# A list scheduler in the kernel sets the order of all work in a cross-covariance attention

## The chip, the cores and the metric

One core of one Trainium2 chip runs the kernel. Its engines are PE (matmul; PEld is its weight load), DVE (vector), ACT (scalar), POOL (GpSimd) and SP, which issues all the DMA transfers. Each engine works through its own instructions in the order in which the program gives them and waits on semaphores for the others. The metric is the device time of one execution in microseconds.

## The reference

Q, K and V have the shape 8 x 12 x 512 x 64 (batch, heads, sequence, dimension) in float32. The attention is over the dimension, not over the sequence: each head has a 64 x 64 matrix.

```python
Q_norm = Q / (np.linalg.norm(Q, axis=-2, keepdims=True) + 1e-10)
K_norm = K / (np.linalg.norm(K, axis=-2, keepdims=True) + 1e-10)
attn = np.einsum('bhnd,bhne->bhde', Q_norm, K_norm)
attn = np.exp(attn - np.max(attn, axis=-1, keepdims=True))
attn = attn / (np.sum(attn, axis=-1, keepdims=True) + 1e-10)
return np.einsum('bhnd,bhde->bhne', V, attn).astype(np.float32)
```

## The kernel before

The 96 heads form 24 units of 4 heads, and two units form a pair `s` (12 pairs). A unit's Q, K or V is one transfer of 512 KB: 128 partitions, 32 for each head, with 16 rows of 64 in each. A pair's result leaves in two stores of 512 KB. That makes 96 transfers, 24 each of Q, K, V and the output, all in SP's queue.

For a unit, DVE casts Q and K to bf16, side by side in one tile (L77). PE multiplies that tile by its own transpose, 64 small matmuls (L89), so that each head's 128 x 128 Gram matrix holds Q^T Q, K^T K and K^T Q. [...] DVE takes the diagonals (L99) and K^T Q (L104) out of it. For a pair, DVE sums the diagonals (L108), GpSimd raises them to the power -1/2 (L110), DVE scales K^T Q by the norms of K (L114), PE transposes the result into the logits (L121, L122), ACT takes the exponential with the norms of Q as its scale (L128) and adds up the rows, and DVE divides (L134, L137), which gives `ab`.

V goes another way. GpSimd casts it to bf16 (L81), PE transposes it in two halves for a pair (L148) through one PSUM buffer, and ACT copies each half to SBUF (L152). Then PE multiplies by `ab` in four groups for a pair (L163), ACT copies each group from PSUM into the tile that is stored (L164), and after every second group SP stores the tile (L72).

The order is written out by hand. The main loop has 28 steps. Step `s` issues the loads of Q and K for unit s + 4 and of V for unit s + 2, then one store of pair s // 2 - 2, and then the compute, where unit s is in its grams, the pair before it in logits to output products, and the pair before that in its last output group. The program order of each engine is the order of these calls:

```python
if s + LA < U:
    load_qk(s + LA)
if s + LA - VLAG < U:
    load_v(s + LA - VLAG)
```

Of the kernel before, what the change touches and what calls it, by code (L numbers as in the profile page):

```python
# [13 lines left out]
D = 64  # L14
T = 16
HU = 4
J = T // 2


@with_exitstack  # L20
def kernel(
# [11 lines left out]
    S = U // 2  # L33

# [9 lines left out]

    const = ctx.enter_context(tc.tile_pool(name="const", bufs=1))
    qp = ctx.enter_context(tc.tile_pool(name="qp", bufs=5))
    vp = ctx.enter_context(tc.tile_pool(name="vp", bufs=4))
    vbp = ctx.enter_context(tc.tile_pool(name="vbp", bufs=4))
    qkp = ctx.enter_context(tc.tile_pool(name="qkp", bufs=3))
    vtp = ctx.enter_context(tc.tile_pool(name="vtp", bufs=2))  # L50
    sop = ctx.enter_context(tc.tile_pool(name="sop", bufs=6))
    small = ctx.enter_context(tc.tile_pool(name="small", bufs=2))
    ps_g = ctx.enter_context(tc.tile_pool(name="ps_g", bufs=1, space=bass.MemoryType.PSUM))
# [4 lines left out]
    qk32, v32, vb, qkb, gram, scr, kq, r8, kqs, lg, ex, ab, vt, so = ({} for _ in range(14))  # L58
    LO, HI = slice(0, D), slice(D, 2 * D)

    def load_qk(u):
        t_ = qk32[u] = qp.tile([128, 2, T, D], F32, name="qk32")
        r = u % 2
        nc.sync.dma_start(out=t_[:, r], in_=Qu[u * 128:(u + 1) * 128])
        nc.sync.dma_start(out=t_[:, 1 - r], in_=Ku[u * 128:(u + 1) * 128])

    def load_v(u):
        t_ = v32[u] = vp.tile([128, T, D], F32, name="v32")
        nc.sync.dma_start(out=t_, in_=Vu[u * 128:(u + 1) * 128])

    def store(s, i):
        nc.sync.dma_start(out=Of[s, i], in_=so[s, i])  # L72

    def cast_qk(u):
        t_ = qkb[u] = qkp.tile([128, T, 2 * D], BF16, name="qkb")
        for x in range(2):
            nc.vector.tensor_copy(t_[:, :, x * D:(x + 1) * D], qk32[u][:, x])  # L77

    def cast_v(u):
        t_ = vb[u] = vbp.tile([128, T, D], BF16, name="vb")  # L80
        nc.gpsimd.tensor_scalar(out=t_, in0=v32[u], scalar1=1.0, scalar2=0.0, op0=ALU.mult, op1=ALU.add)  # L81
# [24 lines left out]
    def norms(s):  # L106
        n2 = small.tile([128, 2 * HU], F32, name="n2")
        nc.vector.tensor_reduce(out=n2, in_=scr[s], axis=mybir.AxisListType.X, op=ALU.add)  # L108
        t_ = r8[s] = small.tile([128, 2 * HU], F32, name="r8")
# [21 lines left out]
    def normalise(s):  # L131
# [3 lines left out]
        a = ab[s] = abs_[s % len(abs_)]  # L135
# [5 lines left out]
    def vtrans(s, k):  # L141

        ps = ps_v.tile([128, 2, J // 2, 128], BF16, name="vps")
# [5 lines left out]
        if k == 0:  # L149
            vt[s] = vtp.tile([128, J, 128, 2], BF16, name="vt")  # L150
        o = vt[s][:, k * (J // 2):(k + 1) * (J // 2)]
        nc.scalar.copy(o.rearrange("p j x c -> p c j x"), ps)  # L152

    def outs(s, x):
        i, k = divmod(x, 2)
        if k == 0:
            so[s, i] = sop.tile([128, 2, J, D], F32, name="so")
        po = ps_o.tile([128, J // 2, 2, D], F32, name="po")
        for j in range(J // 2):
            for e in range(2):  # L160
                h = 2 * i + e
                w = vt[s][:, k * (J // 2) + j, 32 * h:32 * (h + 1), :].rearrange("p x c -> p (x c)")
                nc.tensor.matmul(po[e * D:(e + 1) * D, j].rearrange("p r d -> p (r d)"), w, ab[s][:, h, :])  # L163
        nc.scalar.copy(so[s, i][:, :, k * (J // 2):(k + 1) * (J // 2)].rearrange("p r j d -> p j r d"), po)  # L164

    LA = 4
    VLAG = 2

    for u in range(LA):
        load_qk(u)  # L170
        if u >= VLAG:
            load_v(u - VLAG)

# [10 lines left out]
    for i in range(3):  # L184
# [4 lines left out]
    cast_qk(0)  # L189
    for s in range(U + 4):  # L190
        p, odd = divmod(s, 2)
        if s + LA < U:
            load_qk(s + LA)
        if s + LA - VLAG < U:
            load_v(s + LA - VLAG)

        if odd and 0 <= p - 2 < S:
            store(p - 2, 1)
        if not odd and 0 <= p - 2 < S:
            store(p - 2, 0)  # L200
        if s + 1 < U:
            cast_qk(s + 1)
        if 0 <= s - 1 < U:
            cast_v(s - 1)
        if not odd and 0 <= p - 1 < S:
            scale_k(p - 1)
        if odd and 0 <= p - 1 < S:
            normalise(p - 1)
        if s < U:
            grams(s)  # L210
            squares(s)
        if odd and s < U:
            norms(p)
        if not odd and 0 <= p - 2 < S:
            outs(p - 2, 3)
        if not odd and 0 <= p - 1 < S:
            logits(p - 1)
            exps(p - 1)
            vtrans(p - 1, 0)
        if odd and 0 <= p - 1 < S:  # L220
            vtrans(p - 1, 1)
            for x in range(3):
                outs(p - 1, x)
# [30 lines left out]
```

## Time and profile before

| | |
|---|---|
| median of 3 runs | 140.41 us (140.38 to 140.78) |
| the profiled execution | 141.48 us, of which the span is 139.7 |
| PE, PEld | 84.4 us (60%), 69.6 us (50%) busy |
| DVE | 95.4 us (68%) |
| ACT | 71.9 us (51%) |
| POOL | 50.0 us (36%) |
| DMA | 50.69 MB, 363 GB/s over the span |
| mean granted TensorE clock | 0.82 |

The span is the time from the first to the last instruction of the profiled execution; what lies around it belongs to the launch. A busy share is a mean over the whole span: no engine is busy all the time, and the stretches of the span must be looked at one by one. L12 is line 12 of the kernel before.

### The profile page before, as it was taken

The numbers are of one execution on the slowest core, as the hardware profiler recorded it, in microseconds if no ns is written. First come the engines' busy times: TensorE is split into PE (matmuls) and PEld (weight loads), VectorE is DVE, ScalarE is ACT, GpSimd is POOL, SyncE is SP. The second block draws the span as 40 slices with busy tenths as digits, with TensorE's granted clock in tenths as the row PEclk, the third lists the DMA queues.
The fourth block names the chain that finished last, engine by engine and source line by source line (L and its number), as shares of the span: only waits on it lengthen the run. The fifth ranks groups of instructions, "written<-read, shape, count | busy, mean of one in ns | idle before, by whom it ended". The sixth has DMA issues, their size and how long they took to land.

```text
span 139.7 us, 5665 instructions
## 1 busy us (share of the span) xinstructions
PE 84.4 (60%) x2496; PEld 69.6 (50%) x2496; DVE 95.4 (68%) x183; ACT 71.9 (51%) x169; POOL 50.0 (36%) x45
## 2 busy tenths in 40 slices
PE   0225584795565954656966557946937745966440
PEld 0224473774454843545854446735835634855330
DVE  2347786798798867848797977886795977543200
ACT  0000047657386467344477636447573753865670
POOL 3002542740914705501906407308209209143000
PEclk9999999559999599855699985797797799686555
DMA  4999999999999999999999999999999999707016
GB/s 156 364 409 418 407 409 405 412 407 406 407 412 409 419 406 411 415 412 411 410 418 408 416 409 410 419 413 416 406 415 410 411 413 349 274 22 292 11 69 232
DMA packets 16920, 50.69 MB, mean 363 GB/s; under 512 B 1536, under 2 KB 1536, under 8 KB 16896
## 3 DMA queue, kind: packets, MB, share of 16 engines
q1 hardware_dynamic: 16896, 50.34, 90.8%
q8 instruction: 19, 0.31, 0.9%
q14 instruction: 5, 0.04, 0.1%
HBM read 37.75 MB, written 12.58 MB: 360 GB/s over the span
## 4 chain that ended last, share of the span: by engine, by line
PE 40%; ACT 22%; issue 13%; DVE 10%; POOL 5%; DMA 5%; SPq 1%; POOLq 0%; ACTq 0%
PE gram L89 15%; ACT vt L152 14%; PE po L163 9%; PE vps L148 8%; PE lg L121 7%; ACT ex L128 6%; POOL r L110 5%; DMA qk<-in_K_dram 5%; DVE kqs L114 3%; DVE scr L99 2%; DVE n L108 1%; DVE ab L137 1%; DVE kq L104 1%; ACT L128 1%; ACT so L164 1%
## 5 line engine op out<-in xcount | busy, mean ns | idle before, releaser
L89 PE MATMUL gram<-qkb 32*128 32x128 bf16 x1536 | 37.1, 259 | 21.3 <-issue 10.3
L110 POOL TENSOR_TENSOR r<-n,mhalf 128x8 f32<-128x8 f32 x12 | 23.2, 1932 | 57.6 <-DVE n L108 38.0
L89 PEld LDWEIGHTS <-qkb 32*128 32x128 bf16 x1536 | 30.2, 115 | 23.7 <-issue 10.8
L152 ACT COPY vt<-vps 128x1024 bf16<-128x1024 bf16 x24 | 31.2, 1301 | 16.4 <-PE vps L148 16.4
L164 ACT COPY so<-po 128x512 f32<-128x512 f32 x48 | 26.9, 587 | 22.7 <-PE po L163 22.2
L77 DVE CAST qkb<-qk 128x1024 bf16<-128x1024 f32 x48 | 32.3, 712 | 6.6 <-DMA qk<-in_K_dram 3.8
L163 PE MATMUL po<-ab,vt 128*64 128x128 bf16 x384 | 23.7, 257 | 17.4 <-ACT vt L152 13.3
L81 POOL TENSOR_SCALAR vb<-v 128x1024 bf16<-128x1024 f32 x24 | 25.8, 1078 | 18.6 <-DMA v<-in_V_dram 17.4
L163 PEld LDWEIGHTS <-vt 128*64 128x64 bf16 x384 | 16.3, 130 | 20.5 <-ACT vt L152 15.5
L99 DVE SCALAR_TENSOR_TENSOR scr<-gram,eye 64x256 f32<-64x256 f32 x48 | 20.2, 421 | 7.8 <-PE gram L89 7.3
L148 PE MATMUL vps<-identb,vb 128*64 128x128 bf16 x384 | 18.8, 251 | 8.7 <-ACT vt L152 7.7
L114 DVE TENSOR_TENSOR kqs<-kq,r 128x256 f32<-128x256 f32 x12 | 14.2, 1186 | 12.6 <-POOL r L110 12.6
L148 PEld LDWEIGHTS <-vb 128*64 128x64 bf16 x384 | 14.9, 128 | 12.3 <-issue 10.3
L128 ACT ACTIVATE ex<-lg,r 128x64 f32<-128x64 f32 x48 | 14.4, 311 | 5.7 <-PE lg L122 5.4
L121 PEld LDWEIGHTS lg<-eye,kqs 64*64 64x64 f32 x96 | 9.1, 181 | 9.0 <-DVE kqs L114 8.4
L121 PE MATMUL lg<-eye,kqs 64*64 64x64 f32 x96 | 11.0, 276 | 3.5 <-DVE kqs L114 3.5
L128 ACT ACT_TABLE_LOAD x1 | 1.3, 1283 | 19.3 <-PE lg L122 19.3
L122 PE MATMUL lg<-eye,kqs 64*64 64x64 f32 x96 | 11.0, 276 | 0.0
L137 DVE TENSOR_TENSOR ab<-ex,rinv 64x256 bf16<-64x256 f32 x24 | 10.3, 429 | 0.6
L104 DVE COPY kq<-gram 64x256 f32<-64x256 f32 x24 | 10.0, 419 | 0.4
L128 ACT ACTIVATION_READ_ACCUMULATOR ex<-lg,r 128x1 f32 x48 | 9.7, 202 | 0.0
L122 PEld LDWEIGHTS lg<-eye,kqs 64*64 64x64 f32 x96 | 9.1, 181 | 0.0
(12 smaller groups left out, 12.8 us busy)
## 6 DMA issues: line engine op xcount, KB each, us to landing
qk<-in_Q_dram SPq DMA_DIRECT2D x24, 512.0 KB, 10.1
qk<-in_K_dram SPq DMA_DIRECT2D x24, 512.0 KB, 10.1
v<-in_V_dram SPq DMA_DIRECT2D x24, 512.0 KB, 10.0
out_dram<-so SPq DMA_DIRECT2D x24, 512.0 KB, 10.0
```

What stands on the lines that cost most here:

```text
L77: nc.vector.tensor_copy(t_[:, :, x * D:(x + 1) * D], qk32[u][:, x])
L81: nc.gpsimd.tensor_scalar(out=t_, in0=v32[u], scalar1=1.0, scalar2=0.0, op0=ALU.mult, op1=ALU.add)
L89: nc.tensor.matmul(g[:, h, 0:2 * D], x, x, start=(t == 0), stop=(t == T - 1))
L99: nc.vector.scalar_tensor_tensor(out=scr[s][half, HU * (x ^ r):HU * (x ^ r) + HU], in0=g[half, :, half], scalar=1e-20, in1=eye2[half, None ...
L110: nc.gpsimd.tensor_tensor(out=t_, in0=n2, in1=mhalf, op=ALU.pow)
L121: nc.tensor.matmul(l[LO, h, :], kqs[s][HI, h, :], eye2[HI])
L122: nc.tensor.matmul(l[HI, h, :], kqs[s][LO, h, :], eye2[LO])
L128: nc.scalar.activation(e[:, h, :], lg[s][:, h, :], AF.Exp, scale=r8[s][:, h:h + 1], accum_out=z[:, h:h + 1])
L148: nc.tensor.transpose(ps[r * D:(r + 1) * D, c, j, :], vb[2 * s + r][:, t, :], identb)
L152: nc.scalar.copy(o.rearrange("p j x c -> p c j x"), ps)
L163: nc.tensor.matmul(po[e * D:(e + 1) * D, j].rearrange("p r d -> p (r d)"), w, ab[s][:, h, :])
L164: nc.scalar.copy(so[s, i][:, :, k * (J // 2):(k + 1) * (J // 2)].rearrange("p r j d -> p j r d"), po)
```

## The change

The hand-written loop goes. Every step becomes a piece with a key, the engines on which it may run with a cost in us for each, the pieces that must have ended (`after`), those that must have begun (`behind`), and a rank. A planner in the kernel, when the program is built, repeatedly takes the pieces that may begin within 0.25 us of the earliest one, and of these the one with the lowest rank, and then emits all pieces in the order of their planned beginnings. DMA is modelled as one queue with 8 transfers under way, 2.0 us of flight and 1.27 us for each transfer.

The ranks of transfers go with their unit's number: Q and K at 0.76 u / 24, V at 0.10 + 0.80 v / 24, stores 0.10 behind V's formula. Some buffers are added: V in bf16 6 for 4, transposed V 3 for 2, store tiles 8 for 6. The scaling of K^T Q moves from DVE to GpSimd, into one piece with the power. In the last four pairs (`s >= BOTH`), the copies of transposed V are halved and go to ACT or DVE, as do the copies of the output groups, and V's cast may go to DVE. The last two pairs (`s >= TAIL`) use other PSUM buffers: the Gram tile's four banks are closed after the last squares and opened again as two buffers for transposes and two for products.

```diff
+    HOP = 0.15
+    SLACK = 0.25
+    QUEUE = 8
+    FLIGHT = 2.0
...
+                for eng, cost in engines.items():
+                    begin = max(ready, free.get(eng, 0.7))
+                    if eng == "DMA":
+                        if len(landed) >= self.QUEUE:
+                            begin = max(begin, landed[-self.QUEUE])
+                        done = max(begin + self.FLIGHT, landed[-1] if landed else 0.0) + cost
+                        busy = begin + 0.45
...
+            first = min(b[0] for b in best)
+            begin, rank, key, (_, _, busy, eng, done) = min(
+                (b for b in best if b[0] <= first + self.SLACK), key=lambda b: (b[1], b[0], str(b[2])))
...
+    TAIL = S - 2
+    BOTH = S - 4
...
+    NB = dict(qk=5, v=4, vb=6, qkb=3, vt=3, so=8, sm=2, ab=3)
...
+    def late_pool():
+        if not late:
+            grams_only.close()
+            late["p"] = ctx.enter_context(tc.tile_pool(name="ps_t", bufs=2, space=bass.MemoryType.PSUM))
+        return late["p"]
...
-    def scale_k(s):
         t_ = kqs[s] = small.tile([128, HU, D], F32, name="kqs")
-        nc.vector.tensor_tensor(
+        nc.gpsimd.tensor_tensor(
             out=t_, in0=kq[s], in1=r8[s][:, HU:, None].to_broadcast([128, HU, D]), op=ALU.mult,
         )
...
-    cast_qk(0)
-    for s in range(U + 4):
...
+    QK_PACE, V_FROM, V_PACE, ST_LAG = 0.76, 0.10, 0.80, 0.10
+    def v_at(v):
+        return V_FROM + V_PACE * v / U
...
+        at = QK_PACE * u / U
+        free = [back("cq", u, NB["qk"], 0), back("cq", u, NB["qk"], 1)]
+        piece(("lq", u), {"DMA": X}, free, [back("lk", u, 1)], at, load_qk, u, 0)
+        piece(("lk", u), {"DMA": X}, free, [("lq", u)], at, load_qk, u, 1)
+        piece(("cq", u, 0), {"DVE": 0.70}, [("lq", u), back("gr", u, NB["qkb"])], [back("cq", u, 1, 1)], 10 + u, cast_qk, u, 0)
+        piece(("cq", u, 1), {"DVE": 0.70}, [("lk", u)], [("cq", u, 0)], 10 + u, cast_qk, u, 1)
+        piece(("gr", u), {"PE": 1.6}, [("cq", u, 0), ("cq", u, 1), back("sq", u, 1)], [], 2, grams, u)
+        piece(("sq", u), {"DVE": 1.30}, [("gr", u), back("sc", s, NB["sm"])], [back("sq", u, 1)], 1, squares, u)
...
+        piece(("rd", s), {"DVE": 0.69}, [("sq", 2 * s), ("sq", 2 * s + 1), back("sc", s, NB["sm"])], [], 1, sums, s)
+        piece(("sc", s), {"POOL": 2.4}, [("rd", s), back("lg", s, NB["sm"]), back("ex", s, NB["sm"])], [], 1, powers, s)
+        piece(("lg", s), {"PE": 0.8}, [("sc", s), back("ex", s, 1)], [], 1, logits, s)
+        piece(("ex", s), {"ACT": 2.05}, [("lg", s), back("nm", s, NB["sm"])], [], 1, exps, s)
+        piece(("nm", s), {"DVE": 1.05}, [("ex", s)] + [back("ou", s, NB["ab"], x) for x in range(4)], [], 1, normalise, s)
...
+        piece(("lv", v), {"DMA": X}, [back("cv", v, NB["v"])], [back("lv", v, 1)], v_at(v), load_v, v)
+        piece(("cv", v), {"POOL": 1.05, "DVE": (0.7, 0.2)} if s >= BOTH else {"POOL": 1.05},
+              [("lv", v), back("vt", v // 2, NB["vb"] // 2, 1)], [back("cv", v, 1)], 3 + 0.01 * v, cast_v, v)
...
+            if t:
+                wait = [("vc", s - 1, k, c) for c in halves] if s > TAIL else [("sq", U - 1)]
...
+            piece(("vc", s, k, c), {"ACT": 0.66, "DVE": 0.60} if s >= BOTH else {"ACT": 1.31},
...
+            wait = [("oc", n // 4 + (TAIL if t else 0), n % 4)] if n >= 0 else [("sq", U - 1)] if t else []
+            piece(("ou", s, x), {"PE": 0.5}, [("vc", s, k, c) for c in halves] + [("nm", s)] + wait, order, 3 + 0.01 * s, outs, s, x)
...
+            piece(("oc", s, x), {"ACT": 0.6, "DVE": (0.6, 0.2)} if s >= BOTH else {"ACT": 0.6}, [("ou", s, x)] + free, order, 2 + 0.01 * s, ocopy, s, x)
...
+            piece(("st", s, i), {"DMA": X}, [("oc", s, 2 * i), ("oc", s, 2 * i + 1)], order, v_at(2 * s + i) + ST_LAG, store, s, i)
+    for emit, eng in plan.run():
+        emit(eng)
```

In this code `U` is 24 and `S` 12, and `back(kind, i, n)` names the piece of that kind n numbers earlier, so it stands for a buffer's earlier use. The pieces are `lq`, `lk`, `lv` (loads), `cq`, `cv` (casts), `gr` (grams), `sq` (squares and the copy of K^T Q), `rd` (sums), `sc` (power and scaling), `lg`, `ex`, `nm` (logits, exponentials, division), `vt`, `vc` (transposes of V and their copies), `ou`, `oc` (output products and their copies) and `st` (stores).

## Rows read from the trace of the kernel before

**Rows 1.** The page's second part: 40 equal slices of the span.

```profile
DMA  4999999999999999999999999999999999707016
GB/s 156 364 409 418 407 409 405 412 407 406 407 412 409 419 406 411 415 412 411 410 418 408 416 409 410 419 413 416 406 415 410 411 413 349 274 22 292 11 69 232
```

**Rows 2.** Stretches: length, busy us of five engines, PEclk, DMA share, GB/s.

```profile
0.00:115.00 115.00, 71.06 (x2188) 58.74 (x2190) 86.61 (x167) 58.14 (x138) 43.27 (x40) 0.85 1.01 402
115.00:139.70 24.70, 13.32 (x312) 10.87 (x311) 8.77 (x17) 13.71 (x32) 6.76 (x5) 0.67 0.48 181
...
15.00:115.00 100.00, 67.05 (x2060) 55.25 (x2054) 79.21 (x152) 58.14 (x138) 40.93 (x30) 0.83 1.03 411
...
137.00:138.00 1.00, 0.00 (x0) 0.00 (x0) 0.00 (x0) 0.00 (x0) 0.00 (x0) 0.50 1.01 385
138.00:138.50 0.50, 0.00 (x0) 0.00 (x0) 0.00 (x0) 0.00 (x0) 0.00 (x0) 0.50 0.71 262
```

**Rows 3.** Timeline of SP, 95 us to the end: start, duration, instruction.

```profile
102.29 0.33 SPq L65 DMA_DIRECT2D qk<-in_K_dram  x1
...
108.67 0.33 SPq L69 DMA_DIRECT2D v<-in_V_dram  x1
109.98 26.39 SPq L72 DMA_DIRECT2D out_dram<-so  x7
```

**Rows 4.** The page's sixth part: issues, KB each, median us to landing.

```profile
qk<-in_K_dram SPq DMA_DIRECT2D x24, 512.0 KB, 10.1
```

**Rows 5.** Waits of SP before 108 us, then after: us, times, longest.

```profile
SPq L72 <- ACT so L164: 0.7, 3, 0.4
...
SPq L72 <- ACT so L164: 22.6, 6, 7.5
```

**Rows 6.** Timeline of the tail: start, duration, instruction, idle before it.

```profile
120.00 1.89 PE L89 MATMUL gram<-qkb 32*128 32x128 bf16 x64
...
123.36 0.69 DVE L108 TENSOR_REDUCE n<-scr 128x8 f32<-128x512 f32 x1
124.22 1.64 POOL L110 TENSOR_TENSOR r<-n,mhalf 128x8 f32<-128x8 f32 x1 [4.97 <-DVE n L108]
...
125.83 1.04 POOL L81 TENSOR_SCALAR vb<-v 128x1024 bf16<-128x1024 f32 x1
125.89 1.25 DVE L114 TENSOR_TENSOR kqs<-kq,r 128x256 f32<-128x256 f32 x1 [1.84 <-POOL r L110]
...
129.97 0.85 DVE L137 TENSOR_TENSOR ab<-ex,rinv 64x256 bf16<-64x256 f32 x2
130.96 1.06 PE L148 MATMUL vps<-identb,vb 128*64 128x128 bf16 x16 [1.64 <-ACT vt L152]
...
132.06 1.29 ACT L152 COPY vt<-vps 128x1024 bf16<-128x1024 bf16 x1 [1.15 <-PE vps L148]
...
134.72 0.64 PE L163 MATMUL po<-ab,vt 128*64 128x128 bf16 x8 [0.23 <-ACT so L164]
...
135.40 0.58 ACT L164 COPY so<-po 128x512 f32<-128x512 f32 x1 [0.24 <-PE po L163]
```

**Rows 7.** The same timeline, PE's groups at the full clock.

```profile
115.69 1.07 PE L89 MATMUL gram<-qkb 32*128 32x128 bf16 x64
116.69 0.41 PE L163 MATMUL po<-ab,vt 128*64 128x128 bf16 x7
...
119.43 0.64 PE L148 MATMUL vps<-identb,vb 128*64 128x128 bf16 x16
```

**Rows 8.** Groups by line, and lines L114 and L110 (ns min/median/max).

```profile
L77 DVE CAST qkb<-qk 128x1024 bf16<-128x1024 f32 x48 | 32.3, 712 | 6.6 <-DMA qk<-in_K_dram 3.8
...
L179 POOL TENSOR_TENSOR eye<-ident 128x64 f32<-128x64 f32 x1 | 0.3, 318 | 0.0
...
L114 DVE TENSOR_TENSOR kqs<-kq,r x12: 425/1254/1257, 17.6 to 125.9; 128x256 f32<-128x256 f32 x12
...
L110 POOL TENSOR_TENSOR r<-n,mhalf x12: 1635/1918/2169, 15.6 to 124.2; 128x8 f32<-128x8 f32 x12
```

More of the change, by code (lines that the diff above doesn't have):

```diff
@@ L17, with __init__, add, run @@
 J = T // 2
+LO, HI = slice(0, D), slice(D, 2 * D)
+class Order:
+    HOP = 0.15
+    SLACK = 0.25
+    QUEUE = 8
+    FLIGHT = 2.0
+    def __init__(self):
+        self.pieces = {}
+    def add(self, key, engines, after, behind, rank, emit):
+        after, behind = (tuple(a for a in x if a is not None) for x in (after, behind))
+        self.pieces[key] = (engines, after, behind, rank, emit)
+    def run(self):
+        end, begun, free, landed, order = {}, {}, {}, [], []
+        todo = dict(self.pieces)
+        while todo:
+            best = []
+            for key, (engines, after, behind, rank, _) in todo.items():
+                if any(a not in end for a in after + behind):
+                    continue
+                ready = max([end[a] + self.HOP for a in after] + [begun[a] for a in behind], default=0.7)
+                pick = None
+                for eng, cost in engines.items():
[5 more added lines that the diff above has]
+                        busy = begin + 0.45
+                    else:
+                        bias = 0.0
+                        if isinstance(cost, tuple):
+                            cost, bias = cost
+                        done = busy = begin + cost
+                        done += bias
+                    if pick is None or done < pick[0]:
+                        pick = (done, begin, busy, eng, done if eng == "DMA" else busy)
+                best.append((pick[1], rank, key, pick))
+            first = min(b[0] for b in best)
+            begin, rank, key, (_, _, busy, eng, done) = min(
+                (b for b in best if b[0] <= first + self.SLACK), key=lambda b: (b[1], b[0], str(b[2])))
+            end[key] = done
+            begun[key] = begin
+            free[eng] = busy
+            if eng == "DMA":
+                landed.append(done)
+            order.append((begin, len(order), key, eng))
+            del todo[key]
+        self.end = end
+        self.order = sorted(order)
+        return [(self.pieces[key][4], eng) for _, _, key, eng in self.order]
 @with_exitstack
@@ L56 @@
     ps_o = ctx.enter_context(tc.tile_pool(name="ps_o", bufs=2, space=bass.MemoryType.PSUM))
[L58 to L65, printed above, removed]
+    grams_only = ExitStack()
@@ new lines, with copy @@
+    ps_g = grams_only.enter_context(tc.tile_pool(name="ps_g", bufs=1, space=bass.MemoryType.PSUM))
+    late = {}
+    def late_pool():
[3 more added lines that the diff above has]
+        return late["p"]
+    qk32, v32, vb, qkb, gram, scr, kq, r8, kqs, lg, ex, ab, vps, vt, po, so = ({} for _ in range(16))
+    def copy(eng, o, i):
+        if eng == "ACT":
+            nc.scalar.copy(o, i)
+        elif eng == "DVE":
+            nc.vector.tensor_copy(o, i)
+        else:
+            nc.gpsimd.tensor_scalar(out=o, in0=i, scalar1=1.0, scalar2=0.0, op0=ALU.mult, op1=ALU.add)
@@ L183 @@
     abs_ = []
-    for i in range(3):
+    for i in range(NB["ab"]):
         a = const.tile([128, HU, 2 * D], BF16, name=f"ab{i}")
@@ L187 @@
         abs_.append(a)
-    cast_qk(0)
-    for s in range(U + 4):
[L191 to L223, printed above, removed]
+    plan = Order()
@@ new lines, with piece, back @@
+    X = 1.27
+    QK_PACE, V_FROM, V_PACE, ST_LAG = 0.76, 0.10, 0.80, 0.10
+    def v_at(v):
+        return V_FROM + V_PACE * v / U
+    def piece(key, engines, after, behind, rank, fn, *args):
+        if key[0] in ("cv", "vc", "oc"):
+            plan.add(key, engines, after, behind, rank, lambda eng: fn(eng, *args))
+        else:
+            plan.add(key, engines, after, behind, rank, lambda eng: fn(*args))
+    def back(kind, i, n, *rest):
+        return (kind, i - n, *rest) if i - n >= 0 else None
```

105 lines of the change are left out of this document (70 added, 35 removed).

## The prediction

> **What bounds the kernel now.** I read first the page's slices [rows 1], to find the stretches with different limits. The reader is to see the DMA row at 9 (90% or more) from slice 2 to slice 34 and then broken, 7 0 7 0 1 6, while the GB/s row falls from about 410 to 274, 22, 292, 11, 69, 232. So there are two kernels in one: a stream that the DMA engines set, and a tail of some 22 us that something else sets. The split into stretches gives sizes [rows 2]: 411 GB/s at a share of 1.03 from 15 to 115 us, and 181 GB/s over the last 24.7 us. The traffic is the same 96 transfers of 0.524 MB whatever their order (0.524 MB / 411 GB/s = 1.28 us each). What is left at 115 us is 24.7 us x 181 GB/s = 4.47 MB, or 10.9 us at full rate. The last bytes move at about 138.3 us (a stretch of 0.5 us at 262 where a full one has some 385), 1.4 us before the end. A stream without gaps would so end at 115 + 10.9 + 1.4 = 127.3 us instead of 139.7: **12.4 us is all there is to win.**
>
> Next, why the tail starves. SP's own timeline [rows 3] has the last K load at 102.29 us, the last V load at 108.67, and then nothing but seven stores spread over 26 us. SP's waits [rows 5] say what for: up to 108 us it waited 0.7 us in all for the copies that fill the store buffers, after that 22.6 us. So all loads are in flight by 109 us, and the end is set by how long the compute takes from the last load to the last store. The last K load lands 10.1 us after its issue by the median [rows 4], near 112.4; the last copy into a store buffer ends at 135.40 + 0.58 = 135.98 [rows 6]; from there to the end are 3.7 us (issue, transfer, completion), which any order keeps. Those 23.6 us hold far less work than that, as the chain's rows show [rows 6]: the last gram starts at 120.00, 7.6 us after its data landed (DVE's in-order queue stood behind the scaling of K^T Q and its wait for GpSimd, PE's behind copies), and the last pair's transposes and vt copies (130.96, 132.06) stand behind the exponentials although they need only V, which had long been there.
>
> **The change, part by part.**
>
> *Chain from the last K landing to the last copy.* With nothing queued ahead, by the rows: cast 0.71 [rows 8]; gram 1.07 at the full granted clock [rows 7] or 1.89 at the lower level [rows 6]; squares and Gram copy 1.47 (grams end at 121.89, the reduce starts at 123.36); reduce 0.69; power 1.64 here, 1.92 in the middle of the twelve [rows 8]; scaling, see below; logits, exponentials and reciprocal 2.8 (127.14 to 129.97); the two normalising multiplies 0.85; four groups of output matmuls of 0.41 to 0.64 [rows 6, 7]; the last copy 0.58; nine or ten hand-overs between engines, 0.2 to 1.4 in all. Low ends: 0.71 + 1.07 + 1.47 + 0.69 + 1.64 + 0.32 + 2.8 + 0.85 + 1.64 + 0.58 + 0.2 = 12.0. High ends: 0.71 + 1.89 + 1.47 + 0.69 + 1.92 + 1.28 + 2.8 + 0.85 + 2.56 + 0.58 + 1.4 = 16.2. I take 14.2: the middle, since the granted clock was 0.67 on the mean after 115 us and 0.50 at the very end [rows 2]. Against 23.6 that is **9.4 us less**. The planner earns it by three things: V's transposes and copies of the last pairs come before, not behind, the last exponentials; the last four pairs' copies may go to DVE or ACT; and the last two pairs get two PSUM buffers for transposes in place of one (the four Gram banks, free after the last squares).
>
> *Scaling on GpSimd.* It leaves DVE's queue (12 of these at 0.43 to 1.26 us, 1.25 in the middle, and the waits for the power ahead of them) and joins the power on GpSimd. The trace has no such operation on GpSimd; the nearest row is a two-input one of 128x64 at 0.32 us [rows 8]. Lower end 0.32 (all fixed cost), upper end 4 x 0.32 = 1.28 (all per element). I take 0.8, so 0.45 better than the 1.25 of DVE on the last chain. On DVE it frees 12 x 1.2 = 14 us of 95, in a stretch that the DMA sets: worth nothing there, but the last gram is no longer late behind it. Its cover on GpSimd is the slack beside two V casts of 1.04 per pair: 1.9 + 0.8 + 2.1 = 4.8 us in a pair's 8 x 1.28 = 10.2 us. Without that cover a V cast would be late by 0.8 us, with transfers in flight ten us deep.
>
> [...] The row first: the scaling on DVE took 425 ns at least and 1254 in the middle [rows 8], and in the tail a V cast of 1.04 us on GpSimd starts within 0.1 us of it, so the one engine waits for the other here. [...]
>
> *Q and K lead.* The last K load has 84 transfers ahead of and including it now (48 of Q and K, 21 of V, 15 stores, by the loop's order). In the ranks of the change K of unit 23 has 0.76 x 23 / 24 = 0.728; V loads below that are (0.728 - 0.10) / 0.80 x 24 = 18.8, so 19; stores 15.8, if ready. A store can't go before its copies, which come some 17 us after its V load's issue (10.1 to landing, some 7 for cast, transposes, copies, products), about 3.5 V loads, so 14 to 16 are ready: 81 to 83 transfers, 1 to 3 fewer, 1.3 to 3.8 us earlier. I take one, **1.3 us**, since late stores are sent first by their low ranks. So K lands near 111.1 and the last copy ends at 111.1 + 14.2 = 125.3.
>
> *V trails.* The last V load stays near its place (108.67 + 10.1 = 118.8 [rows 3, 4]; 89th transfer, and 88 or 89 in the new ranks); 117.5 to 118.8. From there cast 0.71 on DVE to 1.04 on GpSimd, transposes 0.64 to 1.06, two half copies of 0.58 (L164's row for the same 512 elements stands for them), four output groups 1.64 to 2.56, a copy 0.58, hand-overs: 5 to 8, so 123 to 126, beside the other chain, not behind it. Both ends meet, as the ranks have it.
>
> *Stores close.* At 115 us some 8 stores are left; those of pairs 8 and 9 need no late data and fill the queue to about 120; pair 10's wait for the last squares (111.1 + 0.71 + 1.9 + 1.5 = 115.2) plus some 4 us. Then the queue may run dry for 1 to 3 us until pair 11's. Eight store buffers for six: no wait of L72's kind for buffers shows [rows 5], worth nothing.
>
> *Fixed order.* It adds waits where the planner's times are off: no more than a row's kind of hand-over (1.15 and 1.64 us in front of the last copy and transposes [rows 6]) on one or two engines. Between 0 and 4 us; I take 0.6, since DVE, freed of GpSimd's waits, has more slack than now.
>
> *Sum.* 125.3 + 3.7 + 0.6 = 129.6 us of span, 2.3 above the stream's bound of 127.3, 10.1 less than now. The profiled execution took 141.48 with its span of 139.7, so 131.4 for one like it; the median of the runs is 1.07 us lower (140.41), which gives 140.41 - 10.1 = **130.3 us**.
>
> **Rivals.** *A: the last two pairs come one after the other.* All their transposes and products wait for the last squares, and the clock is at its lower level. One pair now takes 5.0 us from its second transposes to its last copy (130.96 to 135.98) and some 2.4 for the first half: 7.4. Two in series from 115.2: 130.0, + 3.7 = 133.7 of span, 134.4 in the median. For it: the 0.50 of the tail [rows 2]. Against: the copies go to two engines and the buffers double, so the second pair's transposes run under the first pair's copies.
>
> *B: slower, the queue of SP starves the stream.* Loads and stores share SP's queue in order. A store put closely behind its copy, as the planner does, blocks the loads behind it when the copy is late; then the shortage comes in each of 12 pairs and not once. It decides from 10.5 / 12 = 0.9 us of DMA idle per pair; with 1 us per pair the time is 130.3 + 12 = 142.3. For it: SP waited 22.6 us for those copies where nothing else was left to issue. Against: each issue stands 10.1 us ahead of its landing [rows 4], so a store must be some 8 us late before the engines run dry, and up to 108 us it was late by 0.7 us in total.
>
> *C: Q and K do not lead* (their five buffers or DVE hold them). Then 1.3 us is lost: 131.6, inside the forecast's own range.
>
> **Numbers.** Forecast with C, 127.8 to 133: 0.68. A and mixtures of late engines, 133 to 139.9: 0.20. Within 0.3% of 140.41 (0.4 us, about what a measurement of this kernel tells from no change): 0.04, for a tail that gives everything back. B, slower: 0.08. So faster 0.88, same 0.04, slower 0.08. The low end of the range is the stream's bound, 140.41 - 12.4 = 128.0, a little below for scatter; the high end takes in A's value: 127.8 to 135.0, leaving out some 0.2.
>
> **What would show it.** Right: DMA at 9 through slice 36 or more of 40, one or two broken slices; last K load issued before 102; the scaling on GpSimd at 0.3 to 1.3 us; the last gram within 2 us of its cast; last transposes ahead of the last exponentials; 3.7 us from the last copy to the end. A: output copies of pair 10 end after 121 and PE's idle time behind vt copies over 1 us each. B: SP waits for ACT or DVE copies before 100 us, and GB/s slices under 390 in the middle. The prediction is wrong if the stream has gaps before 110 us, or if the last chain takes over 16 us from the last K landing.

## The result, and the profile after

The changed kernel takes 135.01 us (median of 4 runs, 134.82 to 135.79) beside 140.59 us for the kernel before on the same chip: a ratio of 0.9588 [0.9505, 0.9671], 5.6 us faster. The forecast was 10.1 us faster. The profiled execution took 134.82 us, with a span of 133.0 against the 129.6 worked out ahead, at a mean granted clock of 0.822.

The page's second part, in 40 slices, answers [rows 1]: the DMA row holds a 9 through slice 35, one short of what the forecast asked, and of the last five slices four are below 9 where one or two were forecast; one carries 87 GB/s.

```profile
DMA  4999999999999999999999999999999999972976
GB/s 143 394 424 413 406 410 405 409 408 411 402 406 412 409 411 412 411 410 416 405 414 405 421 408 406 410 418 405 409 416 407 417 411 392 338 288 87 373 278 225
```

Stretches of the kernel after (length, busy us of PE, PEld, DVE, ACT and POOL, granted clock, DMA share, GB/s). The stream is what it was in [rows 2], 410 GB/s; the tail is shorter and fuller. The next fence has the tail of the kernel before from the same instant: 34.70 us at 247 GB/s have become 28.00 us at 306, so the whole gain comes after 105 us.

```profile
15.00:105.00 90.00, 62.21 (x1894) 51.83 (x1884) 67.22 (x136) 49.12 (x127) 44.94 (x38) 0.80 1.03 410
105.00:133.00 28.00, 15.85 (x432) 13.32 (x426) 18.38 (x34) 15.79 (x38) 9.07 (x8) 0.80 0.81 306
115.00:126.50 11.50, 7.97 (x202) 6.84 (x201) 9.42 (x17) 7.53 (x18) 3.29 (x3) 0.85 0.70 260
...
120.00:122.00 2.00, 1.47 (x47) 1.28 (x44) 1.73 (x4) 1.93 (x7) 0.60 (x1) 1.00 0.02 9
```

```profile
105.00:139.70 34.70, 19.86 (x512) 16.12 (x509) 16.12 (x31) 19.20 (x45) 10.85 (x8) 0.72 0.64 247
```

SP's timeline after (start, duration, instruction), to set beside [rows 3]: the last K load leaves at 98.41 and not at 102.29, but the last V load leaves at 112.72 and not at 108.67, since two stores held SP for 4.27 us in front of it.

```profile
98.41 0.55 SPq L145 DMA_DIRECT2D qk<-in_K_dram  x1
...
108.34 4.27 SPq L152 DMA_DIRECT2D out_dram<-so  x2
112.72 0.42 SPq L149 DMA_DIRECT2D v<-in_V_dram  x1
```

The last K transfer landed 10.0 us after its issue and the last V transfer 7.1 us after its own (issues by tile: count, KB, us to landing), so at 108.4 and 119.8. In the kernel before, the last V transfer took 11.3 us from its issue at 108.67 and landed at 120.0: leaving 4 us later, it now lands no later.

```profile
qk<-in_K_dram SPq DMA_DIRECT2D x1, 512.0 KB, 10.0
v<-in_V_dram SPq DMA_DIRECT2D x1, 512.0 KB, 7.1
```

From there the last chain runs over four engines. Each timeline has start, duration, instruction and, in brackets, the idle time before it. DVE:

```profile
109.63 0.74 DVE L137 COPY vt<-vps 128x512 bf16<-128x512 bf16 x1 [0.82 <-ACT vt L135]
110.26 0.83 DVE L180 SCALAR_TENSOR_TENSOR scr<-gram,eye 64x256 f32<-64x256 f32 x2
...
111.47 1.29 DVE L137 COPY so<-po 128x512 f32<-128x512 f32 x2
112.79 1.14 DVE L158 CAST qkb<-qk 128x1024 bf16<-128x1024 f32 x1
...
114.04 0.85 DVE L219 TENSOR_TENSOR ab<-ex,rinv 64x256 bf16<-64x256 f32 x2
114.92 0.73 DVE L137 COPY vt<-vps 128x512 bf16<-128x512 bf16 x1
116.09 0.86 DVE L180 SCALAR_TENSOR_TENSOR scr<-gram,eye 64x256 f32<-64x256 f32 x2 [0.44 <-PE gram L170]
116.99 0.42 DVE L185 COPY kq<-gram 64x256 f32<-64x256 f32 x1
...
120.77 0.68 DVE L137 CAST vb<-v 128x1024 bf16<-128x1024 f32 x1
121.72 1.89 DVE L137 COPY so<-po 128x512 f32<-128x512 f32 x3 [0.27 <-PE po L250]
123.52 0.17 DVE L216 RECIPROCAL rinv<-esum 128x4 f32<-128x4 f32 x1
123.72 0.85 DVE L219 TENSOR_TENSOR ab<-ex,rinv 64x256 bf16<-64x256 f32 x2
...
125.22 0.72 DVE L137 COPY vt<-vps 128x512 bf16<-128x512 bf16 x1
```

PE:

```profile
113.98 0.62 PE L170 MATMUL gram<-qkb 32*128 32x128 bf16 x30 [0.91 <-DVE qkb L158]
115.38 0.68 PE L170 MATMUL gram<-qkb 32*128 32x128 bf16 x34 [0.78 <-issue]
...
117.55 1.92 PE L231 MATMUL vps<-identb,vb 128*64 128x128 bf16 x32 [0.39 <-DVE kq L185]
...
123.88 0.64 PE L231 MATMUL vps<-identb,vb 128*64 128x128 bf16 x16
...
126.75 1.08 PE L250 MATMUL po<-ab,vt 128*64 128x128 bf16 x16 [1.55 <-ACT vt L135]
```

GpSimd and ACT:

```profile
119.99 0.61 POOL L196 TENSOR_TENSOR kqs<-kq,r 128x256 f32<-128x256 f32 x1
```

```profile
120.86 0.58 ACT L135 COPY so<-po 128x512 f32<-128x512 f32 x1
121.44 0.31 ACT L210 ACTIVATE ex<-lg,r 128x64 f32<-128x64 f32 x1
...
125.97 0.73 ACT L135 COPY vt<-vps 128x512 bf16<-128x512 bf16 x1 [1.23 <-DVE vt L137]
...
128.74 0.58 ACT L135 COPY so<-po 128x512 f32<-128x512 f32 x1 [0.24 <-PE po L250]
```

The reader is to see two things in these rows. The first is DVE's order. The cast of the last K could begin at 108.4 and begins at 112.79: DVE first ends earlier casts, waits 0.82 us for ACT and copies a half of transposed V (109.63), and then does the squares of unit 22, the copy of K^T Q and two output copies, all of which its fixed order puts in front. The reciprocal of the last pair could begin at about 122.7, when its exponentials end, and begins at 123.52, behind three output copies. The last V cast, on DVE too, stands at 120.77. DVE is busy for 9.42 of the 11.50 us from 115 to 126.5, and both chains that end the kernel go through it. The second is which of them ends last. The last division ends at 124.57, but the last two half copies of V only begin at 125.22 on DVE, behind that division, and at 125.97 on ACT, behind DVE's. PE waits 1.55 us for them before the last products.

### The profile page after: what moved, and what is told of

Same layout as the page of the kernel before. It is cut to its first block, busy times and chain, and to the rows that moved or that the text cites. A ratio compares the mean times of both kernels' runs of the same rounds, so it can differ in the third digit from the quotient of the medians.

```text
span 133.0 us, 5673 instructions
## 1 busy us (share of the span) xinstructions
PE 83.4 (63%) x2496; PEld 70.0 (53%) x2496; DVE 94.5 (71%) x186; ACT 64.9 (49%) x164; POOL 56.1 (42%) x55
## 4 chain that ended last, share of the span: by engine, by line
DMA 41%; PE 19%; DVE 14%; issue 9%; ACT 8%; POOL 4%; SPq 1%; DVEq 1%; POOLq 1%; ACTq 0%
DMA v<-in_V_dram 15%; DMA qk<-in_K_dram 12%; PE gram L170 9%; DMA qk<-in_Q_dram 8%; DMA out_dram<-so 7%; PE po L250 4%; ACT vt L135 4%; DVE scr L180 4%; DVE qkb L158 3%; PE vps L231 3%; POOL r L194 3%; PE lg L203 2%; ACT so L135 2%; DVE so L137 2%; DVE kq L185 2%
## 5 line engine op out<-in xcount | busy, mean ns | idle before, releaser
L158 DVE CAST qkb<-qk 128x1024 bf16<-128x1024 f32 x48 | 34.8, 761 | 7.4 <-DMA qk<-in_Q_dram 6.4
L135 ACT COPY vt<-vps 128x1024 bf16<-128x1024 bf16 (+1 forms) x26 | 28.2, 1089 | 13.0 <-PE vps L231 9.6
L135 ACT COPY so<-po 128x512 f32<-128x512 f32 x41 | 23.0, 592 | 17.3 <-PE po L250 17.1
L250 PE MATMUL po<-ab,vt 128*64 128x128 bf16 x384 | 21.6, 256 | 11.3 <-ACT vt L135 7.6
L231 PE MATMUL vps<-identb,vb 128*64 128x128 bf16 x384 | 20.1, 261 | 2.9 <-issue 1.8
L231 PEld LDWEIGHTS <-vb 128*64 128x64 bf16 x384 | 16.3, 137 | 4.3 <-issue 2.3
L203 PE MATMUL lg<-eye,kqs 64*64 64x64 f32 x96 | 10.3, 264 | 4.9 <-POOL kqs L196 4.9
L203 PEld LDWEIGHTS lg<-eye,kqs 64*64 64x64 f32 x96 | 8.4, 169 | 6.8 <-POOL kqs L196 5.9
L204 PE MATMUL lg<-eye,kqs 64*64 64x64 f32 x96 | 10.3, 264 | 0.0
L185 DVE COPY kq<-gram 64x256 f32<-64x256 f32 x24 | 10.1, 419 | 0.3
L189 DVE TENSOR_REDUCE n<-scr 128x8 f32<-128x512 f32 x12 | 8.2, 687 | 0.4
L196 POOL TENSOR_TENSOR kqs<-kq,r 128x256 f32<-128x256 f32 x12 | 8.0, 669 | 0.9
## 6 DMA issues: line engine op xcount, KB each, us to landing
qk<-in_Q_dram SPq DMA_DIRECT2D x24, 512.0 KB, 10.1
qk<-in_K_dram SPq DMA_DIRECT2D x24, 512.0 KB, 10.1
v<-in_V_dram SPq DMA_DIRECT2D x24, 512.0 KB, 10.1
```

What stands on the lines that cost most here:

```text
L135: nc.scalar.copy(o, i)
L158: nc.vector.tensor_copy(qkb[u][:, :, y * D:(y + 1) * D], qk32[u][:, y])
L185: nc.vector.tensor_copy(kq[s][k], g[k, :, q])
L203: nc.tensor.matmul(l[LO, h, :], kqs[s][HI, h, :], eye2[HI])
L231: nc.tensor.transpose(ps[r * D:(r + 1) * D, c, j, :], vb[2 * s + r][:, t, :], identb)
L250: nc.tensor.matmul(po[s, x][e * D:(e + 1) * D, j].rearrange("p r d -> p (r d)"), w, ab[s][:, h, :])
```

## The experiments

The theory (F): the change gains because the last loads of Q and K lead and because the work of the last pairs is spread over two engines and more buffers; what was missing of the forecast is lost in DVE's and SP's fixed orders. Rivals: the halved copies lose it, since the two halves of one copy run one after the other (T); the V loads are too late (V); the planner's costs are wrong (P). The last column below is against the changed kernel, worked out from the ratios at 140.6 us: the first eight against its ratio of 0.9588, the later ones against the 0.9611 of its second series, which shared their chip. By the intervals of the two ratios such a difference is uncertain by 1 to 1.5 us. Timelines differ from one execution to the next too: in e12's, of the same program as the changed kernel's, the last K load leaves 1.0 us later (99.45) and the last squares end 0.7 us later (118.07). So a difference of a microsecond between two timelines shows nothing by itself.

| run | edit | us | ratio to before | us against the changed kernel |
|---|---|---|---|---|
| e1 | V copies whole | 134.96 | 0.9542 [0.9477, 0.9606] | -0.6 |
| e2 | last copies on ACT alone | 139.80 | 0.9875 [0.9818, 0.9933] | +4.0 |
| e3 | scaling back on DVE | 137.97 | 0.9751 [0.9691, 0.9811] | +2.3 |
| e4 | before, with scaling on GpSimd | 139.89 | 0.9869 [0.9789, 0.9950] | (-1.8 against before) |
| e5 | Q and K don't lead | 140.34 | 1.0007 [0.9969, 1.0045] | +5.9 |
| e6 | PSUM not divided anew | 139.23 | 0.9903 [0.9867, 0.9939] | +4.4 |
| e7 | eight V buffers | 135.91 | 0.9669 [0.9611, 0.9726] | +1.1 |
| e8 | measured costs in the planner | 139.11 | 0.9894 [0.9820, 0.9968] | +4.3 |
| e9 | V later | 138.55 | 0.9830 [0.9756, 0.9904] | +3.1 |
| e10 | last unit's work moved ahead | 138.04 | 0.9782 [0.9705, 0.9859] | +2.4 |
| e11 | Q and K earlier, V later | 140.26 | 0.9945 [0.9907, 0.9984] | +4.7 |
| e12 | changed kernel again | 135.16 | 0.9611 [0.9549, 0.9673] | 0 |

### Parts of the change undone, one at a time (e1 to e6)

e1, the halves of a V copy whole again, by whichever of the two engines:

```diff
-            halves = (0, 1) if s >= BOTH else (None,)
+            halves = (None,)
-{"ACT": 0.66, "DVE": 0.60} if s >= BOTH else {"ACT": 1.31}
+{"ACT": 1.31, "DVE": 1.25} if s >= BOTH else {"ACT": 1.31}
```

> The changed kernel, but in the last four pairs each half of transposed V is copied whole by one engine (ACT 1.31 us or DVE 1.25, the planner's choice) instead of in two parts that the plan gives to both engines. [...] Rival R (loads land where they land and the copies are not what sets the end): no change, 134.6 to 135.4. Rival Q (a whole copy of 1.3 us is a longer step than two parts): 135.5 to 137.

The difference is within the intervals. T falls: the halves do run one after the other (below), but without them the time is the same. In e1's order the last K cast also ends at 109.83, 4.1 us earlier than in the changed kernel, and the last squares at 116.49, 0.9 us earlier; that gains nothing either.

e2, the last four pairs' copies and casts on one engine each, as in the other pairs:

```diff
-    BOTH = S - 4
+    BOTH = S + 1
```

> The changed kernel with the last copies on ACT alone, as in all other pairs, and V's casts on GpSimd alone: the part of the change called last copies on two engines is undone, and DVE keeps only its chain for Q and K. Theory T (DVE stands on both chains and its fixed order puts copies ahead of the last K cast, which started at 112.8 with its data there at about 108.5): the last K cast starts before 110, the exponentials of the last pair before 119, and the time is 132 to 135, no slower than the changed kernel. Rival R (ACT alone has 4 x 0.59 + 2 x 1.31 + 1.2 = 6.2 us per pair and falls behind over the last four pairs): 136 to 139.

ACT's timeline of e2, three rows of its tail. After the exponentials it copies without a pause until 130.8, the last copy ending at 133.42 against 129.32.

```profile
120.84 2.48 ACT L135 COPY vt<-vps 128x1024 bf16<-128x1024 bf16 x2
...
129.50 1.30 ACT L135 COPY vt<-vps 128x1024 bf16<-128x1024 bf16 x1
...
132.84 0.58 ACT L135 COPY so<-po 128x512 f32<-128x512 f32 x1 [0.24 <-PE po L250]
```

Stretch from 114 us to the last copy, first of e2, then of the kernel after: about 19 to 20 us of work on DVE and ACT together in both, 2.86 + 16.07 in e2 and 10.34 + 9.84 in the other, and the length follows the fuller engine.

```profile
114.00:133.50 19.50, 11.87 (x226) 9.86 (x225) 2.86 (x7) 16.07 (x29) 4.27 (x4) 0.75 0.55 207
```

```profile
114.00:129.40 15.40, 10.29 (x256) 8.60 (x256) 10.34 (x20) 9.84 (x22) 3.29 (x3) 0.80 0.73 265
```

DVE's timeline of e2 has its last division here. It ends at 122.13, where that of the changed kernel ends at 124.57. So the attention of the last pair came 2.4 us earlier and the end 4 us later: copies set the end, not that chain alone.

```profile
121.28 0.85 DVE L219 TENSOR_TENSOR ab<-ex,rinv 64x256 bf16<-64x256 f32 x2
```

e3, the scaling as a piece of its own on DVE:

```diff
+        piece(("pw", s), {"POOL": 1.9}, ..., powers, s)
+        piece(("sc", s), {"DVE": 0.85}, [("pw", s), back("lg", s, NB["sm"])], [], 1, scale_k, s)
-        nc.gpsimd.tensor_tensor(
+        nc.vector.tensor_tensor(
```

> The changed kernel with the scaling of K^T Q back on DVE, as a piece of its own in the plan (0.85 us, after the power). Theory T (the gain comes from the order of the tail; the scaling is 0.67 us on GpSimd against 1.25 on DVE on the last chain): 135.0 to 136.3. Rival S (freeing DVE of the scaling and its waits is what brings most of the gain): 138 to 140.

The power ended at 120.57 (GpSimd's row: 118.65 1.92). DVE's timeline of e3 shows a V cast in front of the last scaling, which starts at 121.42 and ends 1.2 us later than GpSimd's 120.60 in the kernel after, though it takes only 0.42 us. Of these 1.2 us 0.85 are the time behind the cast and 0.66 a power that ended later (119.91 in the kernel after), less 0.2 for the shorter operation: it is the queue that costs, not the operation. The rest of the 2.3 us isn't traced.

```profile
120.82 0.68 DVE L137 CAST vb<-v 128x1024 bf16<-128x1024 f32 x1
121.42 0.42 DVE L198 TENSOR_TENSOR kqs<-kq,r 128x256 f32<-128x256 f32 x1
```

e4, the same part alone, put into the kernel before:

```diff
-        nc.vector.tensor_tensor(
+        nc.gpsimd.tensor_tensor(
-            scale_k(p - 1)
```

> The kernel before with one part of the change alone: the scaling of K^T Q on GpSimd, right behind the power; the hand-written order stays. Theory T: the last chain loses 0.6 us and DVE's queue no longer stands behind the power in front of the last squares, so 138.5 to 140.2. Rival S (this part brings most of the gain): 135.5 to 137.5.

Alone it gains 1.8 us (0.7 to 3.0 by the interval). GpSimd's timeline of e4 has the last scaling end at 126.16; in [rows 6] it ended at 125.89 + 1.25 = 127.14. Of these 0.98 us, 0.64 are the shorter operation and the rest an earlier start. The spans of the two profiled executions differ by no more (138.7 and 139.7); the other 0.8 of the 1.8 lies within the interval.

```profile
125.55 0.61 POOL L112 TENSOR_TENSOR kqs<-kq,r 128x256 f32<-128x256 f32 x1
```

e5, the ranks of Q and K as slow as those of the stream:

```diff
-    QK_PACE, V_FROM, V_PACE, ST_LAG = 0.76, 0.10, 0.80, 0.10
+    QK_PACE, V_FROM, V_PACE, ST_LAG = 0.84, 0.10, 0.80, 0.10
```

> The changed kernel with Q and K ranked at 0.84 u / 24 instead of 0.76 (V and stores as they are), so that the last K load stands about 5 transfers later in SP's queue: the lead of Q and K is undone. Theory T (the last pair's Q and K chain and its V chain end together in the changed kernel, so a K that lands 4 to 6 us later sets the end): 137 to 139.5. Rival R (the last chain is V's, and Q and K have slack; the prediction priced their lead at 1.3 us): 134.5 to 136.3.

SP's timeline of e5 has the last K load 8.3 us later than the changed kernel and 4.4 us later than the kernel before, so this is more than an undoing. All of the gain is gone, with every other part in place (in the new order that the planner makes of them).

```profile
106.68 1.10 SPq L145 DMA_DIRECT2D qk<-in_K_dram  x1
```

e6, the Gram tile's four banks kept to the end:

```diff
-    TAIL = S - 2
+    TAIL = S
```

> The changed kernel without the second PSUM pool: the last two pairs use the same one buffer for transposes and two for products as all other pairs, and no longer wait for the last squares. Theory T (two buffers let the second half's transposes run under the first half's copies): 136 to 138. Rival R (the wait of pair 10 for the last squares costs as much as the second buffer saves): 134 to 135.8.

4.4 us slower, so taking out the second set of PSUM buffers costs as much as taking out the second copy engine, although their opening makes pair 10's transposes wait for the last squares (PE's row at 117.55 above).

The costs of undoing, 4.0 + 2.3 + 5.9 + 4.4, add up to 16.6 us, three times the gain, so they are no shares of it. That each part works only with the others in place is one reading. Another is that each of these edits also makes the planner put out another order: e8 below takes no part out and loses 4.3 us by its order alone. The runs don't tell the two apart; only in e2, e3 and e5 does a trace show the loss, or a part of it.

### What could have got back the missing 4.7 us (e7 to e11)

e7 tests V, with eight buffers for V, so that its last load need not wait for a buffer:

```diff
-    NB = dict(qk=5, v=4, vb=6, qkb=3, vt=3, so=8, sm=2, ab=3)
+    NB = dict(qk=5, v=8, vb=6, qkb=3, vt=3, so=8, sm=2, ab=3)
```

> The changed kernel with eight buffers for V in float32 instead of four, one number. The last V load went out at 112.7 us, behind a store that waited for its copy and behind the cast of V19, whose buffer it takes. Theory V (the last V load's landing near 119 starts the last chain): it goes out by 108, lands by 117, and the time falls to 132.5 to 134. Rival T (the copies in the fixed order of the last pairs set the end, V has time): 134.4 to 135.6, no change.

SP's timeline of e7 has the last V load 2.8 us earlier than 112.72. But it took 10.1 us to land and not 7.1, so it landed at 120.0, when it did in the changed kernel (119.8). The landing that V asks about did not move, and e7 doesn't test V.

```profile
109.88 0.42 SPq L149 DMA_DIRECT2D v<-in_V_dram  x1
```

```profile
v<-in_V_dram SPq DMA_DIRECT2D x1, 512.0 KB, 10.1
```

The nearest to a test are e2 and e3, where the last V load landed at 118.4 and 118.6: there the last copy came 15.0 and 14.1 us behind it, against 9.5 in the changed kernel. So an earlier landing doesn't do by itself; what it would be worth in the changed kernel's order stays open.

e8 tests P, with the durations of the changed kernel's trace as the planner's costs:

```diff
-    X = 1.27
+    X = 1.29
-{"POOL": 2.4}   {"ACT": 2.05}   {"PE": 1.6}   {"DVE": 0.70}
+{"POOL": 2.6}   {"ACT": 1.25}   {"PE": 1.4}   {"DVE": 0.74}
-{"ACT": 0.66, "DVE": 0.60}   {"ACT": 0.6, "DVE": (0.6, 0.2)}
+{"ACT": 0.74, "DVE": 0.74}   {"ACT": 0.6, "DVE": (0.69, 0.2)}
```

> The changed kernel with the planner's costs set to what its trace shows: 1.29 us per transfer instead of 1.27, exponentials 1.25 instead of 2.05, power and scaling 2.6 instead of 2.4, casts 0.74, grams 1.4, half copies 0.74, DVE's output copies 0.69; nothing else. Theory P (the order is planned for a stream that is 3 us ahead of the real one by the last K load, and the tail pays for it in waits): 132 to 134. Rival N (the order that comes out is as good as the other one; the tail is long for the work that is left in it): 134.4 to 136.

Truer costs gave a worse order. In SP's timeline of e8 the last K load leaves 4.2 us later than in the changed kernel and the last V load 3.1 us later. P falls as I put it: it isn't enough that the costs be true.

```profile
102.65 0.52 SPq L145 DMA_DIRECT2D qk<-in_K_dram  x1
...
115.77 0.41 SPq L149 DMA_DIRECT2D v<-in_V_dram  x1
```

e9 lets V wait longer:

```diff
-... = 0.76, 0.10, 0.80, 0.10
+... = 0.76, 0.14, 0.80, 0.10
```

> The changed kernel with V (and the stores behind it) ranked from 0.14 instead of 0.10, one number: V and stores trail more, and the last K load stands some 3 transfers earlier in the queue than in the changed kernel. Theory K (the last pairs' work hangs on the last squares: the last two pairs' V work waits for them too, through the PSUM banks, so the end follows the last K load about one for one): the last K load goes out by 96 and the time is 131.5 to 133.8. Rival V (V's work of the last pairs is as late as K's, and trails further now): 135 to 137.

The last K load leaves at 96.17, 2.2 us earlier, but the last squares end only 0.6 earlier (the Gram copy 116.37 0.42 for 116.99 0.42), the last two V loads leave at 112.20 to 114.08, the last half copy of V ends 4.1 us later (130.78 for 126.70), and the kernel is 3.1 us slower.

e10 undoes by hand the delay found above. The last K's cast, gram, squares, sums, power and scaling go ahead of what stood in front of them:

```diff
+    put(("cq", 23, 1), ("vc", 8, 1, 1))
+    put(("gr", 23), ("ou", 8, 3))
+    put(("sq", 23), ("nm", 10))
+    put(("rd", 11), ("nm", 10))
+    put(("sc", 11), ("cv", 22))
```

> The changed kernel's own order, in which only five pieces of the last unit and pair are put ahead of copies for the stores: the last K cast (it started at 112.8 with its data there at about 108.5), its grams, its squares, the last sums and the last power. Theory K: the last squares end 2 to 3.5 us sooner than at 117.4 and the time is 132 to 133.8. Rival C (the copies that these pieces now go ahead of belong to pair 9, whose stores feed the queue, and are late in their place): 134.4 to 136.

DVE's timeline of e10: the cast starts at 109.53, 3.3 us earlier than after, as meant, and the squares start at 115.99, only 0.10 earlier. Part of that is the execution: its last K landed at 109.5, 1.1 us later. Counted from that landing to the end of the last squares, it is 7.8 us in e10, 9.0 in the changed kernel and 8.5 in e12.

```profile
109.53 0.69 DVE L158 CAST qkb<-qk 128x1024 bf16<-128x1024 f32 x1 [0.50 <-DMA qk<-in_K_dram]
...
115.99 0.86 DVE L180 SCALAR_TENSOR_TENSOR scr<-gram,eye 64x256 f32<-64x256 f32 x2 [2.00 <-PE gram L170]
...
118.13 0.85 DVE L219 TENSOR_TENSOR ab<-ex,rinv 64x256 bf16<-64x256 f32 x2
119.01 0.73 DVE L137 COPY vt<-vps 128x512 bf16<-128x512 bf16 x1
```

PE's timeline of e10 says why the rest was not won: the gram starts at 112.82, 2.6 us after its cast (PE first does the gram of unit 22, the logits of pair 10, at 0.31 us for most of their matmuls where those of pair 11 take 0.22, and output products), breaks off after 54 of its 64 matmuls, and goes on at 115.61 without waiting for any engine.

```profile
112.82 0.95 PE L170 MATMUL gram<-qkb 32*128 32x128 bf16 x54
115.61 0.34 PE L170 MATMUL gram<-qkb 32*128 32x128 bf16 x10 [1.84 <-issue]
```

DVE, in order, stood still for 2.00 us in front of the squares, and pair 10's division behind them slid from 114.04 to 118.13, the half copy behind that from 114.92 to 119.01. A stall on one engine became 4.1 us on work that had nothing to do with it.

e11 asks for still more lead:

```diff
-... = 0.76, 0.10, 0.80, 0.10
+... = 0.70, 0.14, 0.80, 0.06
```

> The changed kernel with Q and K at 0.70, V from 0.14 and stores 0.06 behind it: the last K load some 5 transfers earlier than in the changed kernel, the last V load no later than one transfer. Theory K: 130.5 to 133. Rival V (past a point V's work after the last V load, some 10 us, sets the end): 133.5 to 136.

The GB/s row of e11's page (40 slices) shows rival B most clearly: gaps in the middle of the stream, 348 and 354, 367 and 382, then 268 and 304. (e8 has single slices of 375 and 377 there, e9 of 382 and 360, e12 one of 377.) And V's side ends this run: the last squares end at 112.79, 4.6 us earlier than in the changed kernel, and the last division 2.3 us earlier, but the last V load lands at 122.6 and the last half copy of V ends at 132.57.

```profile
GB/s 165 349 402 416 409 415 405 408 403 414 403 404 405 409 416 409 413 412 405 411 348 354 416 418 367 382 413 409 414 411 411 268 304 351 379 191 43 304 335 233
```

e12 is the changed kernel again, on the chip of e9 to e11.

> The changed kernel once more, on the chip of these runs, so that they stand beside it: 134.3 to 136, a ratio of 0.952 to 0.966 to the kernel before.

No version beat the changed kernel; e1 equals it.

## Why the prediction was right or wrong

**Right: the frame.** The stream kept its rate up to 105 us, the traffic is the same, and the last copy to the end takes 133.0 - 129.32 = 3.7 us, as forecast. The gain comes whole from the tail and in the direction given. By the ratio, 0.9588 of the 140.41 us from which I started, the time is 134.6, inside the range; the median itself, 135.01, lies a hundredth above its end, which I had put there for A. That it comes out there is in part luck, since the two errors that follow have opposite signs. No stretch before 110 us has a gap, so B is wrong here, though the first half of its sign came true. Before 100 us SP waited 14.0 us for ACT's copies (us, times, longest), where [rows 5] had 0.7; the longest of these waits is far under the 8 us that I had named as harmful.

```profile
SPq L152 <- ACT so L135: 14.0, 9, 2.8
```

**Too low: the lead of Q and K.** I priced it at 1.3 us, from counting transfers ahead of the last K load. The load left 102.29 - 98.41 = 3.9 us earlier (2.8 in e12) and landed at 108.4, not 111.1. By SP's timeline 81 transfers stand ahead of and including it, 19 loads of V and 14 stores among them: the low end of my 81 to 83, of which I had taken the high one. e5 puts this load 8.3 us later and loses 5.9 us, 0.7 for each; at that rate the 3.9 us of lead are worth 2.8, an estimate. So C (1.3 us lost) was priced too cheap.

**Wrong: "Fixed order", 0.6 us.** This is the step that failed. From the landing of the last K to the last copy I had 14.2 + 0.6 = 14.8 us; measured are 129.32 - 108.4 = 20.9, beyond the 16 that I had named as the sign of a wrong prediction. Up to the last division my terms came to some 11.4 with the hand-overs (middle values); measured are 124.57 - 108.4 = 16.2, of which 4.4 are the cast waiting in DVE's queue, 0.4 its longer duration, 0.8 the gram's break, and 0.8 the reciprocal behind output copies. The rest, 9.8, is less than I forecast: the operations were not priced too low, their places in the queues were left out. From the last division to the last copy I had some 3.4 us; measured are 4.75, since half copies of V stand behind the division on DVE. I had bounded the term between 0 and 4 by one hand-over on one or two engines, on the ground that DVE would have slack without the scaling. In the tail it has none: the same change gives it copies of V, copies of output and V casts, and leaves it busy for 9.42 of 11.50 us; from 105 us on it has 18.38 us of work in 28.00 us, where it had 16.12 in 34.70. I counted what leaves DVE over the whole span and not what comes to it in the last 20 us. That this delay is a loss which could simply be taken back is not shown: e10 moved the cast 3.3 us and the squares 0.1, and in e1 the last K cast ended 4.1 us earlier and the time was the same.

**Wrong: V trails.** I had V's chain end beside the other one; it ends behind it. The last V load left at 112.72, not near 108.67: of the 4.27 us in which SP stood at two stores in front of it, 3.4 were a wait for one of DVE's output copies, as SP's waits from 108 to 113 us show.

```profile
SPq L152 <- DVE so L137: 3.4, 1, 3.4
```

That delay cost nearly nothing: the load landed at 119.8, 1.0 us above my 117.5 to 118.8 and no later than in the kernel before. From there to the last copy are 9.5 us, not 5 to 8. The last pair's transposes were to come ahead of the last exponentials, the first of the three things by which the planner was to earn its gain; they come behind them (121.96 and 123.88, against 121.44), and two half copies of V come behind the last division.

**Right in length, not in place: stores close.** The queue runs dry once for some 3 us, forecast 1 to 3: the rate is 9 GB/s from 120 to 122 us, until ACT's copy at 120.86 ends at 121.44 and the store behind it goes. But that store is pair 9's first, for whose copy SP waited 7.1 us, and not one of pair 11. I had said that pair 9's stores need no late data and fill the queue to about 120, so the length came out right by luck.

**Right in duration, too low in worth: the scaling.** The page's group of L196 after has 669 ns on the mean, the last one 0.61; I took 0.8 between 0.32 and 1.28. The last one is 1.4 times DVE's shortest, 425 ns. In the kernel before, eleven of DVE's twelve scalings began 0.05 or 0.06 us behind a V cast on GpSimd and took 1.25 to 1.26; the twelfth, at 17.65, began 0.03 ahead of the cast and took 0.42. On GpSimd the two that began beside casts on DVE, at 26.45 and, the slowest of the tail, at 108.33, took 0.95, so 0.34 more than the other ten. What I called worth nothing, DVE's freed queue, is not nothing: moving the scaling back costs 2.3 us (e3) for a forecast of 0.45, and 0.85 of these the trace shows as time behind a V cast.

**Rival A.** Its 133.7 us of span is the nearest number, and half of its mechanism is there: pair 10's transposes do wait for the last squares (117.55), and pair 10's last output copy ends after 125, behind A's sign of 121. But from the last squares at 117.41 to the last copy are 11.9 us for two pairs, not A's 14.8, so they do overlap; A's squares came at 115.2. Its time is right by two errors of opposite sign.

**The sum.** 2.7 us gained by the earlier landing against 6.1 lost behind it make the 3.4 us between 129.6 and 133.0. The other 1.3 us of the miss (135.01 - 130.3 = 4.7) are the 1.07 by which the profiled execution before lay above its median, which I took off, while that of after lies 0.2 below its own.

**Open.** Whether any order of this work gets nearer to the stream's bound of 127.3 is not settled, nor what an earlier landing of the last V would be worth. Moving the ranks either way, truer costs, and moving one chain by hand all lost time; that the order given sits on a narrow optimum fits all of them, but no search was made. How e8's costs led to later loads isn't traced further.

## What to carry to other kernels

When a change balances work between engines, add up for the tail alone what each in-order engine gets, and ask of each instruction on the last chain what stands in front of it in its queue: here the operations took less than their price and the queues cost 6 us that had none. A schedule fixed ahead turns a delay of one engine into delays on others (in e10 a standstill of 2.00 us on DVE became 4.1 us for pair 10's division), so bound its cost by the work queued around the critical instruction, not by a hand-over. And test parts by undoing each, but beside an edit that takes no part out and only changes the order: where that alone costs as much (4.3 us in e8), the cost of undoing a part is not yet its worth.

## What the runs showed of the hardware

**PE breaks off at fixed places of its program.** The last gram breaks after 30 matmuls in the changed kernel and after 54 in e10, where it stands 24 matmuls earlier in PE's order (8 output products and 16 transposes were passed): 30 + 24 = 54, the same place. Counted by matmuls in the trace, the breaks of PE over 0.2 us that are put down to issue lie in the changed kernel behind 607, 735, 863, 991, 1119, 1246, 1630, 1886, 2014 and 2270 of them: to within one, multiples of 128 apart, or 256 instructions with the weight loads. The kernel before has twelve such breaks, behind 479, 607, 735, 863, 991, 1119, 1503, 1631, 1759, 2015, 2143 and 2271 matmuls: the same grid. The page's third part has a queue of the kind instruction, here after: 19 packets and 0.31 MB, so 16 KB each. In the changed kernel's trace such a packet takes 0.9 to 1.1 us, and each of these ten breaks ends 2.3 to 2.6 us after one began (the packet at 112.90, PE again at 115.38). The breaks are not rare:

```profile
L170 PE MATMUL gram<-qkb 32*128 32x128 bf16 x1536 | 37.7, 263 | 26.3 <-DVE qkb L158 15.0 <-issue 8.2 <-DVE kq L185 3.1
```

That is 8.2 us of idle time in front of gram matmuls, beside operands that were ready. On the last chain the break cost 0.78 us after and 1.84 in e10. Whether PE waits for the packet, and why a packet begins when it does, isn't shown.

**Two halves of one copy don't run side by side.** ACT and DVE each take one half of transposed V from the same PSUM tile, at 0.73 us; the planner has them at once. A group of waits of the kernel after (us, times, longest):

```profile
ACT vt L135 <- DVE vt L137: 3.3, 3, 1.2
```

So waits keep the halves apart here; what they are there for, the trace doesn't show. On the last chain such a wait is 1.23 us long (ACT at 125.97), and yet e1, without halves, is no faster beyond its interval.
